# A prefix log-sum-exp on one core: from two consecutive time steps per partition to one, with Exp and Ln issued by pairs of row blocks

## The chip, the core and the metric

The kernel runs on one core of a Trainium2 chip. Its engines work side by side and meet only at semaphores: TensorE (PE, matmul, with its weight loads as PEld), VectorE (DVE), ScalarE (ACT, which evaluates Exp and Ln), GpSimd (POOL) and SyncE (SP); the last two issue the transfers here. The metric is the device time of one execution in microseconds (us). The kernel before takes 1290.47 us, the median of three runs (1289.72 to 1290.6). All durations below come from one profiled execution of it, unless something else is said.

## The reference

The input x has shape 4 x 4096 x 4128 (batch, time, feature), float32. Along time the reference keeps a running log of a sum of exponentials, for each batch and feature by itself:

```python
out[:, 0, :] = x[:, 0, :].copy()
for t in range(1, S):
    mx = np.maximum(out[:, t - 1, :], x[:, t, :])
    out[:, t, :] = mx + np.log(np.exp(out[:, t - 1, :] - mx) + np.exp(x[:, t, :] - mx))
```

So out[t] = log(exp(x[0]) + ... + exp(x[t])). The input is 270.5 MB, the output as much.

## The kernel before

The kernel computes exp(x), then a prefix sum over time, then the logarithm. It works in blocks of 256 time steps by all 4128 features, 64 blocks in all: 16 blocks for each of the 4 batches. A block lies in SBUF as a tile `xt` of 128 partitions x 2 x 4128: partition p holds the time steps 2p and 2p+1, which are neighbours in memory, so a transfer moves one run of 33,024 bytes per partition. SP issues the load (L134).

ACT turns the whole tile into fp16 exponentials `et` with one instruction of 8256 elements (L138). `scan` then handles the *preceding* block. The features are cut into four chunks of 1024 columns and a tail of 32. For each chunk one PSUM tile `pt` (128 x 1024 float32; the pool `pmain` has three) is filled by matmuls of 512 columns, all recorded at L79 since a helper `mm` issues them. The matmul contracts over partitions, so a triangular matrix as weights makes a prefix sum over time. `head(c)` adds `incl` times the even steps, `excl` times the odd steps and, except in the first block of a batch, `last` times `carry[c]`. That is the sum up to each even step. Ln of it goes into `xt` (L97). `second(c)` adds `ident` times the odd steps into the same `pt`, which makes the sum up to each odd step. Ln of that goes into `xt` too (L104), and DVE copies `pt` to fp16 as the new `carry[c]` (L105). `last` picks row 127 of the carry, the sum up to the end of the block. The tail has a PSUM tile `qt` of its own, one Ln for both steps (L123) and one copy (L124). POOL then issues the store of `xt` to the output (L125): the result is written over x in the same tile. `xt` has five buffers, so a load waits for the store that empties its buffer.

The order on each engine is the program's own order (`manual_schedule`). Inside a block it is head(0), head(1), second(0), head(2), second(1), head(3), second(2), tail matmuls, second(3), tail Ln. On ACT one period is therefore: Exp of block k+1, then eight Ln of 1024 columns and the tail Ln of block k. [...] each period has two ACT_TABLE_LOAD.

A copy at L105 waits for the Ln that reads the same `pt`, and the next matmul into that buffer waits for the copy.

Of the kernel before, what the change touches and what calls it, by code (L numbers as in the profile page):

```python
# [1 line left out]

# [4 lines left out]

FP32 = mybir.dt.float32
FP16 = mybir.dt.float16
ACT = mybir.ActivationFunctionType  # L10
P = 128
R = 2
CH = 1024
MM = 512


def _constants(nc, pool):


    def tri(base, name):  # L20
        t = pool.tile([P, P], FP16, name=name)
        nc.gpsimd.memset(t, 1.0)

        nc.gpsimd.affine_select(
            out=t, in_=t, pattern=[[1, P]], compare_op=mybir.AluOpType.is_ge,
            fill=0.0, base=base, channel_multiplier=-1,
        )
        return t

    def ones_where_zero(base, mult, step, name):  # L30
        t = pool.tile([P, P], FP16, name=name)
        nc.gpsimd.memset(t, 0.0)
        nc.gpsimd.affine_select(  # L33
            out=t, in_=t, pattern=[[step, P]], compare_op=mybir.AluOpType.not_equal,
            fill=1.0, base=base, channel_multiplier=mult,
        )
        return t

    return (
        tri(0, "incl"),  # L40
        tri(-1, "excl"),
        ones_where_zero(0, 1, -1, "ident"),
        ones_where_zero(-(P - 1), 1, 0, "last"),
    )


@with_exitstack
def kernel(
    ctx: ExitStack,
    tc: tile.TileContext,  # L50
    x: bass.AP,
    out: bass.AP,
):

    nc = tc.nc
    B, S, D = x.shape
    rows = P * R
    n_t = S // rows  # L60
    assert S % rows == 0
    n_main = D // CH
    tail = D - n_main * CH
    t0 = n_main * CH

    consts = ctx.enter_context(tc.tile_pool(name="consts", bufs=1))
    incl, excl, ident, last = _constants(nc, consts)

    xpool = ctx.enter_context(tc.tile_pool(name="xpool", bufs=5))
    epool = ctx.enter_context(tc.tile_pool(name="epool", bufs=2))  # L70
    cpool = ctx.enter_context(tc.tile_pool(name="cpool", bufs=1))
    pmain = ctx.enter_context(tc.tile_pool(name="pmain", bufs=3, space=bass.MemoryType.PSUM))
    ptail = ctx.enter_context(tc.tile_pool(name="ptail", bufs=2, space=bass.MemoryType.PSUM))

    carry = [cpool.tile([P, CH], FP16, name=f"carry{c}") for c in range(n_main)]
    carry_t = cpool.tile([P, tail], FP16, name="carry_t") if tail else None

    def mm(pt, w, rhs, start, stop):
        nc.tensor.matmul(pt, lhsT=w, rhs=rhs, start=start, stop=stop, skip_group_check=True)  # L79

    def scan(b, k, xt, et):
        first = k == 0

        def head(c):
            pt = pmain.tile([P, CH], FP32, name="pt")
            for s in range(0, CH, MM):
                o = pt[:, s:s + MM]
                seg = slice(c * CH + s, c * CH + s + MM)
                mm(o, incl, et[:, 0, seg], True, False)
            for s in range(0, CH, MM):  # L90
                o = pt[:, s:s + MM]
                seg = slice(c * CH + s, c * CH + s + MM)
                mm(o, excl, et[:, 1, seg], False, first)
            if not first:
                for s in range(0, CH, MM):
                    mm(pt[:, s:s + MM], last, carry[c][:, s:s + MM], False, True)
            nc.scalar.activation(xt[:, 0, c * CH:(c + 1) * CH], pt, ACT.Ln)  # L97
            return pt

        def second(c, pt):  # L100
            for s in range(0, CH, MM):
                seg = slice(c * CH + s, c * CH + s + MM)
                mm(pt[:, s:s + MM], ident, et[:, 1, seg], False, True)
            nc.scalar.activation(xt[:, 1, c * CH:(c + 1) * CH], pt, ACT.Ln)  # L104
            nc.vector.tensor_copy(carry[c], pt)  # L105

        prev = None
        for c in range(n_main):
            pt = head(c)
            if prev is not None:  # L110
                second(c - 1, prev)
            prev = pt
        if tail:
            qt = ptail.tile([P, R, tail], FP32, name="qt")
            seg = slice(t0, D)
            for j in range(R):
                mm(qt[:, j, :], incl, et[:, 0, seg], j == 0, False)
                mm(qt[:, j, :], incl if j else excl, et[:, 1, seg], False, first)
                if not first:
                    mm(qt[:, j, :], last, carry_t, False, True)  # L120
        second(n_main - 1, prev)
        if tail:
            nc.scalar.activation(xt[:, :, t0:D], qt, ACT.Ln)  # L123
            nc.vector.tensor_copy(carry_t, qt[:, 1, :])  # L124
        nc.gpsimd.dma_start(  # L125
            out=out[b, k * rows:(k + 1) * rows, :].rearrange("(p j) d -> p j d", j=R), in_=xt,
        )

    ctx.enter_context(tc.manual_schedule())
    work = [(b, k) for b in range(B) for k in range(n_t)]  # L130
    pending = None
    for b, k in work:
        xt = xpool.tile([P, R, D], FP32, name="xt")
        nc.sync.dma_start(  # L134
            out=xt, in_=x[b, k * rows:(k + 1) * rows, :].rearrange("(p j) d -> p j d", j=R),
        )
        et = epool.tile([P, R, D], FP16, name="et")
        nc.scalar.activation(et, xt, ACT.Exp)  # L138
        if pending is not None:
            scan(*pending)  # L140
        pending = (b, k, xt, et)
    scan(*pending)


# [1 line left out]
_INS = ['x']  # L146
_OUTS = [((4, 4096, 4128), 'float32')]


# [23 lines left out]
```

## Time and profile before

| what | value |
|---|---|
| median of three runs | 1290.47 us |
| the profiled execution: its own time, and its span | 1290.47 us, 1288.7 us |
| ACT busy | 1117.1 us, 87% of the span |
| PE busy | 624.2 us, 48% |
| DVE busy | 313.8 us, 24% |
| moved by DMA | 541.48 MB, mean 420 GB/s |
| first Exp starts, first Ln starts | 13.38 us, 31.54 us |
| third and last Exp start | 41.49 us, 1246.09 us |
| last Ln ends | 1273.10 us |

The span runs from the first to the last instruction, and the execution's own time is 1.8 us longer. "Busy" counts the time in which an engine executes; matmuls are pipelined and their ends are modelled, so a busy PE is not a PE at its peak. The granted clock (PEclk) is the share of its full speed that PE was allowed. A line such as "L105" is a line of the kernel.

### The profile page before, as it was taken

The page shows a single profiled execution, that of the slowest core. Times are in us where ns is not written, and L with a number is a line of the kernel's source. Part 1 is how long each engine was busy: PE and PEld are TensorE (multiplying, and loading weights), DVE is VectorE, ACT ScalarE, POOL GpSimd, SP SyncE. Part 2 cuts the span into 40 slices and gives each one's busy share as a digit, 9 for nine tenths or more (in the row PEclk, how much of TensorE's full clock was granted, in tenths as well). Part 3 has the DMA queues.
Part 4 walks back from the last instruction along what each step waited for, and adds up shares of the span by engine and source line. Part 5 has one row for each costly group of instructions (what it writes and reads, how often), then busy time and mean ns, then how long its engine had stood idle before and what let it go on. Part 6 is the DMA issues. An engine that isn't in the chain of part 4 may idle for free.

```text
span 1288.7 us, 6563 instructions
## 1 busy us (share of the span) xinstructions
PE 624.2 (48%) x2392; PEld 246.8 (19%) x2392; DVE 313.8 (24%) x320; ACT 1117.1 (87%) x766; POOL 36.0 (3%) x76
## 2 busy tenths in 40 slices
PE   1544644545446446455455464464553544644543
PEld 0211211212112112122122121121221211211211
DVE  0322312223223122132232231222222322312223
ACT  5889899898898898998998989989989889889894
POOL 0000000000000000000000000000000000000000
PEclk9877778778677777786777777777867777778777
DMA  9999999999999999999999999999999999999966
GB/s 407 417 415 431 433 419 429 433 422 428 434 432 429 423 426 429 422 434 428 426 426 433 424 431 431 434 432 430 427 432 424 426 435 429 432 421 432 430 299 263
DMA packets 18464, 541.48 MB, mean 420 GB/s; under 512 B 2048, under 2 KB 2048, under 8 KB 2048
## 3 DMA queue, kind: packets, MB, share of 16 engines
q0 software_dynamic: 9216, 270.54, 49.3%
q1 hardware_dynamic: 9216, 270.54, 49.0%
q8 instruction: 18, 0.29, 0.1%
q14 instruction: 14, 0.11, 0.0%
HBM read 270.53 MB, written 270.53 MB: 420 GB/s over the span
## 4 chain that ended last, share of the span: by engine, by line
ACT 60%; PE 35%; issue 2%; DMA 2%; DVE 0%; DVEq 0%; SPq 0%; ACTq 0%
PE pt L79 35%; ACT et L138 34%; ACT xt L97 11%; ACT L97 6%; ACT L138 6%; ACT xt L104 2%; DMA xt<-in_x_dram 2%; ACT xt L123 1%; DVE carry L105 0%; DVEq L168 0%; SPq L134 0%; DVE carry_t L124 0%; ACTq L97 0%; DVEq L124 0%
## 5 line engine op out<-in xcount | busy, mean ns | idle before, releaser
L105 DVE CAST carry<-pt 128x1024 f16<-128x1024 f32 x256 | 307.5, 1222 | 960.8 <-ACT xt L104 960.8
L79 PE MATMUL pt<-et,ident 128*128 128x512 f16 x512 | 202.2, 486 | 606.4 <-ACT xt L97 606.4
L138 ACT ACTIVATE et<-xt 128x8256 f16<-128x8256 f32 x64 | 453.3, 7082 | 14.7 <-DMA xt<-in_x_dram 14.0
L97 ACT ACTIVATE xt<-pt 128x1024 f32<-128x1024 f32 x256 | 255.2, 1022 | 126.6 <-PE pt L79 125.8
L104 ACT ACTIVATE xt<-pt 128x1024 f32<-128x1024 f32 x256 | 254.9, 1026 | 11.7 <-PE pt L79 11.7
L79 PE MATMUL pt<-et,incl 128*128 128x512 f16 x512 | 200.7, 482 | 41.2 <-DVE carry L105 20.7
L79 PE MATMUL pt<-et,excl 128*128 128x512 f16 x512 | 193.7, 468 | 0.0
L79 PEld LDWEIGHTS <-ident 128*128 128x128 f16 x512 | 55.7, 109 | 684.8 <-issue 660.3
L79 PE MATMUL pt<-carry,last 128*128 128x512 f16 x480 | 166.4, 433 | 0.0
L79 PEld LDWEIGHTS <-incl 128*128 128x128 f16 x704 | 75.5, 114 | 155.9 <-issue 121.3
L79 PEld LDWEIGHTS <-excl 128*128 128x128 f16 x576 | 66.8, 116 | 101.2 <-issue 57.4
L138 ACT ACT_TABLE_LOAD x63 | 80.8, 1283 | 1.9 <-PEq L157 0.8
L97 ACT ACT_TABLE_LOAD x63 | 80.8, 1283 | 1.1
L79 PEld LDWEIGHTS <-last 128*128 128x128 f16 x600 | 64.9, 110 | 82.6 <-issue 46.6
L125 POOL DMA_DIRECT2D out_dram<-xt x64 | 34.2, 534 | 1237.3 <-ACT xt L123 1237.3
L79 PE MATMUL qt<-et,incl 128*128 128x32 f16 x192 | 17.9, 178 | 0.0
L123 ACT ACTIVATE xt<-qt 128x64 f32<-128x64 f32 x64 | 16.0, 251 | 0.0
L79 PE MATMUL qt<-carry_t,last 128*128 128x32 f16 x120 | 15.1, 176 | 0.0
L124 DVE CAST carry_t<-qt 128x32 f16<-128x32 f32 x64 | 11.6, 181 | 0.0
L79 PE MATMUL qt<-et,excl 128*128 128x32 f16 x64 | 11.3, 177 | 0.0
L33 POOL TENSOR_SCALAR_AFFINE_SELECT ident<-ident 128x128 f16<-128x128 f16 x1 | 0.3, 288 | 0.0
L33 POOL TENSOR_SCALAR_AFFINE_SELECT last<-last 128x128 f16<-128x128 f16 x1 | 0.3, 288 | 0.0
(10 smaller groups left out, 1.8 us busy)
## 6 DMA issues: line engine op xcount, KB each, us to landing
xt<-in_x_dram SPq DMA_DIRECT2D x64, 4128.0 KB, 24.3
out_dram<-xt POOLq DMA_DIRECT2D x64, 4128.0 KB, 23.6
```

What stands on the lines that cost most here:

```text
L33: nc.gpsimd.affine_select(out=t, in_=t, pattern=[[step, P]], compare_op=mybir.AluOpType.not_equal, fill=1.0, base=base, channel_multiplier ...
L79: nc.tensor.matmul(pt, lhsT=w, rhs=rhs, start=start, stop=stop, skip_group_check=True)
L97: nc.scalar.activation(xt[:, 0, c * CH:(c + 1) * CH], pt, ACT.Ln)
L104: nc.scalar.activation(xt[:, 1, c * CH:(c + 1) * CH], pt, ACT.Ln)
L105: nc.vector.tensor_copy(carry[c], pt)
L123: nc.scalar.activation(xt[:, :, t0:D], qt, ACT.Ln)
L124: nc.vector.tensor_copy(carry_t, qt[:, 1, :])
L125: nc.gpsimd.dma_start(out=out[b, k * rows:(k + 1) * rows, :].rearrange("(p j) d -> p j d", j=R), in_=xt,)
L138: nc.scalar.activation(et, xt, ACT.Exp)
```

## The change

A block is now 128 time steps, one per partition, so a tile is 128 x 4128, a transfer moves one run of 16,512 bytes per partition, and there are 128 blocks (32 for each batch). `excl` and `ident` are gone: `incl` times `et` plus `last` times `carry` is the whole sum. A `pt` is filled once by four matmuls, read by one Ln and by one copy to the carry. To keep the number of table loads, two blocks form a group: ACT does two Exp, then the eight Ln and two tail Ln of the preceding group. `xt` has eight buffers of half the size, `et` five. `pmain` keeps three buffers. Stores are issued after each block of 128.

```diff
-R = 2
+G = 2
...
-    rows = P * R
+    rows = P
...
-    xpool = ctx.enter_context(tc.tile_pool(name="xpool", bufs=5))
-    epool = ctx.enter_context(tc.tile_pool(name="epool", bufs=2))
+    xpool = ctx.enter_context(tc.tile_pool(name="xpool", bufs=8))
+    epool = ctx.enter_context(tc.tile_pool(name="epool", bufs=5))
...
-        def head(c):
+        for c in range(n_main):
             pt = pmain.tile([P, CH], FP32, name="pt")
             for s in range(0, CH, MM):
-                o = pt[:, s:s + MM]
                 seg = slice(c * CH + s, c * CH + s + MM)
-                mm(o, incl, et[:, 0, seg], True, False)
-            for s in range(0, CH, MM):
-                o = pt[:, s:s + MM]
-                seg = slice(c * CH + s, c * CH + s + MM)
-                mm(o, excl, et[:, 1, seg], False, first)
+                mm(pt[:, s:s + MM], incl, et[:, seg], True, first)
             if not first:
                 for s in range(0, CH, MM):
                     mm(pt[:, s:s + MM], last, carry[c][:, s:s + MM], False, True)
-            nc.scalar.activation(xt[:, 0, c * CH:(c + 1) * CH], pt, ACT.Ln)
-            return pt
-
-        def second(c, pt):
-            for s in range(0, CH, MM):
-                seg = slice(c * CH + s, c * CH + s + MM)
-                mm(pt[:, s:s + MM], ident, et[:, 1, seg], False, True)
-            nc.scalar.activation(xt[:, 1, c * CH:(c + 1) * CH], pt, ACT.Ln)
+            nc.scalar.activation(xt[:, c * CH:(c + 1) * CH], pt, ACT.Ln)
             nc.vector.tensor_copy(carry[c], pt)
...
         if tail:
-            qt = ptail.tile([P, R, tail], FP32, name="qt")
...
+            qt = ptail.tile([P, tail], FP32, name="qt")
+            mm(qt, incl, et[:, t0:D], True, first)
+            if not first:
+                mm(qt, last, carry_t, False, True)
+            nc.scalar.activation(xt[:, t0:D], qt, ACT.Ln)
+            nc.vector.tensor_copy(carry_t, qt)
+        nc.gpsimd.dma_start(out=out[b, k * rows:(k + 1) * rows, :], in_=xt)
...
-    pending = None
-    for b, k in work:
-        xt = xpool.tile([P, R, D], FP32, name="xt")
...
+    pending = []
+    for g in range(0, len(work), G):
+        group = []
+        for b, k in work[g:g + G]:
+            xt = xpool.tile([P, D], FP32, name="xt")
+            nc.sync.dma_start(out=xt, in_=x[b, k * rows:(k + 1) * rows, :])
+            et = epool.tile([P, D], FP16, name="et")
+            nc.scalar.activation(et, xt, ACT.Exp)
+            group.append((b, k, xt, et))
+        for p in pending:
+            scan(*p)
+        pending = group
+    for p in pending:
+        scan(*p)
```

More of the change, by code (lines that the diff above doesn't have):

```diff
@@ L40, in _constants @@
         tri(0, "incl"),
-        tri(-1, "excl"),
-        ones_where_zero(0, 1, -1, "ident"),
         ones_where_zero(-(P - 1), 1, 0, "last"),
@@ L66 @@
     consts = ctx.enter_context(tc.tile_pool(name="consts", bufs=1))
-    incl, excl, ident, last = _constants(nc, consts)
-    xpool = ctx.enter_context(tc.tile_pool(name="xpool", bufs=5))
-    epool = ctx.enter_context(tc.tile_pool(name="epool", bufs=2))
+    incl, last = _constants(nc, consts)
+    xpool = ctx.enter_context(tc.tile_pool(name="xpool", bufs=8))
+    epool = ctx.enter_context(tc.tile_pool(name="epool", bufs=5))
     cpool = ctx.enter_context(tc.tile_pool(name="cpool", bufs=1))
@@ L107, in scan @@
[L107 to L112, printed above, removed]
-        if tail:
-            qt = ptail.tile([P, R, tail], FP32, name="qt")
[L115 to L127, printed above, removed]
+            nc.scalar.activation(xt[:, c * CH:(c + 1) * CH], pt, ACT.Ln)
+            nc.vector.tensor_copy(carry[c], pt)
+        if tail:
+            qt = ptail.tile([P, tail], FP32, name="qt")
[4 more added lines that the diff above has]
+            nc.vector.tensor_copy(carry_t, qt)
@@ L129 @@
+        nc.gpsimd.dma_start(out=out[b, k * rows:(k + 1) * rows, :], in_=xt)
     ctx.enter_context(tc.manual_schedule())
     work = [(b, k) for b in range(B) for k in range(n_t)]
-    pending = None
-    for b, k in work:
-        xt = xpool.tile([P, R, D], FP32, name="xt")
[L134 to L141, printed above, removed]
@@ L142 @@
-    scan(*pending)
+    pending = []
[12 more added lines that the diff above has]
+        scan(*p)
```

## The prediction

> **What bounds the kernel now.** I read the page first. ACT is busy for 87% of the span and the DMA engines for over 90% in nearly every slice, so either could be the bound.
>
> ```profile
> DMA  9999999999999999999999999999999999999966
> ACT 60%; PE 35%; issue 2%; DMA 2%; DVE 0%; DVEq 0%; SPq 0%; ACTq 0%
> L105 DVE CAST carry<-pt 128x1024 f16<-128x1024 f32 x256 | 307.5, 1222 | 960.8 <-ACT xt L104 960.8
> L138 ACT ACTIVATE et<-xt 128x8256 f16<-128x8256 f32 x64 | 453.3, 7082 | 14.7 <-DMA xt<-in_x_dram 14.0
> L97 ACT ACTIVATE xt<-pt 128x1024 f32<-128x1024 f32 x256 | 255.2, 1022 | 126.6 <-PE pt L79 125.8
> ```
>
> The chain that ended last is ACT and PE; DMA has 2% of it. A group line gives busy us, mean ns of one instruction, then the idle time before it and its releaser. Next, the waits (total us, times, longest):
>
> ```profile
> ACT xt L97 <- PE pt L79: 125.8, 113, 1.5
> ACT et L138 <- DMA xt<-in_x_dram: 14.0, 2, 11.3
> ```
>
> An Exp waits for a load only twice, both at the start. So loads come in time, and a period is set by ACT and its waits for PE. One period in order of time (start, duration; idle before in brackets):
>
> ```profile
> 594.50 7.08 ACT L138 ACTIVATE et<-xt 128x8256 f16<-128x8256 f32 x1
> ...
> 602.90 1.94 ACT L97 ACTIVATE xt<-pt 128x1024 f32<-128x1024 f32 x2
> 603.97 1.01 PE L79 MATMUL pt<-et,ident 128*128 128x512 f16 x2 [9.05 <-ACT xt L97]
> ...
> 607.58 1.02 ACT L97 ACTIVATE xt<-pt 128x1024 f32<-128x1024 f32 x1 [1.54 <-PE pt L79]
> ...
> 610.46 1.02 ACT L97 ACTIVATE xt<-pt 128x1024 f32<-128x1024 f32 x1 [0.94 <-PE pt L79]
> ...
> 612.43 2.36 DVE L105 CAST carry<-pt 128x1024 f16<-128x1024 f32 x2 [1.66 <-ACT xt L104]
> ```
>
> Three `pt` are filled during Exp, so the Ln phase starts at once, then ACT waits for refills. Two Ln in a row take 1.94, so the second adds 0.92; two copies take 2.36, so the second adds 1.14. Early in the burst two matmuls of 512 take 1.06 (0.43 apart), later 0.59 (0.215 apart): PE is cold after the 9 us of Exp. Whole periods (length, PE busy, granted clock, DMA share, GB/s) show what that costs:
>
> ```profile
> 614.74:635.10 20.36, 10.49 (x39) 0.75 1.01 430
> 635.10:653.94 18.84, 8.42 (x36) 0.82 1.01 421
> 653.94:673.48 19.54, 8.76 (x32) 0.74 1.00 426
> ```
>
> ACT issues the same work in each, yet the length moves with the granted clock. The Exp starts give the repeating sequence 18.84, 19.54, 20.00, 20.24, 20.36. In the clock's own record it changes only at multiples of 3.413 us: cold 0.5, warm 1.0. It turns warm at the end of a window in which PE had work for over about 0.765 (0.76 didn't, 0.77 did) and cold after an idle one.
>
> **What the Trainium skill says.** "TensorE: Matmul & The Clock Gate", Part 1 (What's actually happening), has a free-running window of 3413 ns after which a busy PE goes from half to full clock; this trace agrees. "PSUM — Partial Sum Buffer", PSUM bank collisions raise a hardware error, says that two engines, two readers included, must not touch one bank at once. That is why a copy follows its Ln; the copies here start 0.04 us after it. "DMA: Bandwidth & Descriptors", Why small descriptors are slow, names about 3 cycles per packet, so halving 33 KB rows should cost little. Here a row of 33,024 bytes holds an engine 1.222 us, and the trace's few 8,192-byte packets mostly 0.309 us: about 0.007 us each beyond the bytes.
>
> **The change, part by part (per 256 steps; before against after).**
>
> *ACT.* Exp: a 1024 Ln takes 1.022 and the 8256 Exp 7.082, about 0.838 ns an element, so an Exp of 4128 takes about 3.64; two, overlapping by 0.10, take 7.18, or +0.10. Ln: still eight. Tail: one of 64 (0.245) becomes two of 32 at about 0.215, +0.09 with overlap. Table loads: still two. Bare ACT period: about +0.2 us.
>
> *PE.* 32 matmuls of 512 before (8 each of `incl`, `excl`, `last`, `ident`), 32 after (16 `incl`, 16 `last`); tails 6 to 4. No saving.
>
> *DVE.* Eight copies of 1.222 where there were four, +4.9 us: 9.3 us back to back with both tail copies. Before, a buffer served two Ln for one copy. Now each Ln has a copy behind it that holds the buffer: the Ln phase becomes paced by refill, Ln, copy round three buffers.
>
> *The Ln phase, step by step.* Let 0 be the start of the first Exp. Exp end at 7.18, table load 7.19 to 8.47, three prefilled Ln start at 8.49, 9.41 and 10.33. Copies end at 10.77, 11.91 and 13.05. PE starts chunk 4 at 10.83, when the first buffer is free. Cold, four matmuls issue in 1.71, and the last lands 0.16 later.
> - chunk 4 lands 12.70, Ln 12.73 (could start 11.25: waits 1.48); the tail Ln follows at 13.65.
> - chunk 5 starts on PE at 12.59, lands 14.46, Ln 14.49 (waits 0.72).
> - chunk 6 starts 14.30, lands 16.17, Ln 16.20 (waits 0.79).
> - If PE is warm from about 16.1, chunk 7 starts 16.01 and lands 17.07, Ln 17.12; chunk 8 waits for chunk 5's copy (15.55 to 16.77), lands 17.93, Ln 18.04; no further wait.
> - Tail Ln ends 19.18, table load ends 20.47. Period: 20.48, with 2.99 us of waits where the sampled period before has about 2.7.
>
> PE turns warm 2.61 us (0.765 of a window) to 6.02 us after its burst starts at 10.83, as the burst falls on the windows. Earliest, chunk 5 lands 14.04, and chunks 7 and 8 wait for copies: period about 19.9. Latest, chunk 7 lands 17.45 and chunk 8 18.32: 20.85. Before, the same swing is 18.84 to 20.36.
>
> *Where it settles.* Six windows are 20.48 us. A shorter period starts the next burst earlier against the windows, so warmth comes later in it and the period grows; a longer one does the reverse. Before, even the longest (20.36) is under 20.48, so the phase never rests and the sequence climbs and falls back: mean 19.75 ((1246.09 - 41.49) / 61). After, 20.48 lies between 19.9 and 20.85, where the drift stops, with warmth 5.2 us after the burst starts. The period should lock there. The first blocks of a batch, without carry matmuls, disturb it for a few periods, with no net sum.
>
> *DMA.* Sixteen rows of 1.222 per engine become 32 of about 0.615: 19.55 to about 19.7 us bare; measured with its stalls the mix ran at 421 to 430 GB/s, so 8.454 MB take 19.7 to 20.1 and about 0.1 more after. It hides under 20.48. The buffers hold four groups, not five, but stores leave in halves and the load behind each starts sooner. POOL and SP issue 128 transfers instead of 64; an issue takes 0.53 and 0.33, and neither queue holds compute.
>
> *Ends.* First Exp: half of the load's 9.78 us, 13.38 - 4.89 = 8.5. Four Exps paced by loads of 4.9: the fourth runs 23.2 to 26.8, first Ln at 28.1 (before 31.54); an Ln phase and table load of about 11.6 bring the third group's Exp to 39.7. Plus 61 x 20.48 = 1249.3: last group's Exp at 1289.0. Its predecessor's Ln phase ends 19.2 later, and the last eight chunks follow, paced by copies, in about 10.9: 1319.1. The last store is half as long: 15.6 (1288.7 - 1273.1) less 4.9 is 10.7. Span 1329.8; with 1.8 around it, as in the profiled execution, whose time is the median: 1331.6. I say **1331**.
>
> **Rivals.** *No lock:* the phase keeps drifting between 19.9 and 20.85, mean about 20.3: 61 x 0.18 = 11 less, 1320. For it: before drifts so. Against: 20.48 is well inside my range; my terms would have to be 0.4 too long.
>
> *Slower still:* eight copies beside Ln and matmuls lengthen one another in PSUM, or a 16.5 KB packet costs over 0.64 us, so that DMA is the bound. At 20.8 a period it gives 1331 + 61 x 0.32 = 1350. Against: copies keep 1.22 beside Ln today, and 8 KB packets show little overhead.
>
> *Not slower:* PE stays warm through Exp, because prefills wait for the last copies and shorten its idle stretch. Then chunk 4 lands at 11.8, the copy chain alone sets about 19.0, and DMA at 19.7 becomes the bound: 1331 - 61 x 0.78 = 1283. The last prefill starts after the last copy, at about 0.3 us of the next period, and lasts 1.1 at most; the next burst is at 10.83, so over 9 us of idleness remain, over two windows. It decides from a period of 19.9 downward, where the 8 us saved at the ends are spent; I don't expect it.
>
> *The change doesn't do what it says:* ACT, PE and DVE orders are fixed by hand, so no.
>
> **How the numbers follow.** Lock 0.73 (own range 1325 to 1338), no lock 0.13, slower still 0.09, not slower 0.05. Leaving out the fast rival and part of the slow one, the range is 1309 to 1347. About 0.2% (2.6 us) is what the measurement tells from no change. Faster 0.04, same 0.02, slower 0.94: only the third rival ends at or below 1293.
>
> **What would show it.** Right: Exp starts 20.48 apart for long stretches; ACT waiting for PE near 3 us a group (1.5, then twice 0.7 to 0.8); DVE near 650 us; the mean clock near 0.75; no Exp waiting for a load after the start. Wrong: periods near 19.7 with Exp waiting for loads; a clock at 1.0 during Exp; copies well over 1.22; Ln waits spread over all five refilled chunks.

## The result, and the profile after

The kernel after takes 1327.99 us (median of four runs, 1326.83 to 1329.16) against 1290.24 us, now the median of four runs of the kernel before: a ratio of 1.0293, 95% interval 1.0275 to 1.0311, so 38 us slower. The prediction was 1331, with 1309 to 1347 as its range.

The page of the kernel after, the lines that answer to those shown of before:

```profile
DMA  9999999999999999999999999999999999999986
ACT 56%; PE 26%; DVE 12%; issue 3%; DMA 2%; DVEq 0%; SPq 0%; ACTq 0%
L89 DVE CAST carry<-pt 128x1024 f16<-128x1024 f32 x512 | 601.7, 1219 | 703.1 <-ACT xt L88 702.8
L88 ACT ACTIVATE xt<-pt 128x1024 f32<-128x1024 f32 x512 | 499.9, 1023 | 169.4 <-PE qt L76 88.5
L108 ACT ACTIVATE et<-xt 128x4128 f16<-128x4128 f32 x128 | 459.5, 3635 | 11.0 <-DMA xt<-in_x_dram 10.3
```

Each copy costs what it cost before (1219 ns, 1222 before), and there are twice as many. DVE, which had 0% of the chain that ended last, now has 12% of it. The total wait of the Ln instructions rose from 138.3 us (126.6 at L97 and 11.7 at L104) to 169.4 us. Exp still waits for loads only at the start.

The waits of the kernel after (total us, times, longest) show the new link of the chain:

```profile
PE pt L76 <- DVE carry L89: 647.6, 138, 15.6
ACT xt L88 <- PE qt L76: 88.5, 78, 1.4
ACT xt L88 <- ACT xt L95: 44.2, 60, 1.0
ACT xt L88 <- PE pt L76: 34.8, 59, 1.4
ACT et L108 <- DMA xt<-in_x_dram: 10.3, 4, 6.5
```

Before, PE waited for Ln (606.4 us) and for copies only 20.7 us. Now it waits for copies. The second and third lines are waits for PE as well: the releaser named is the last event seen, a tail matmul or a tail Ln that came just before, while the instruction that waits is a 1024 Ln whose chunk was being filled. One Ln phase in order of time (kernel after):

```profile
640.17 2.85 ACT L88 ACTIVATE xt<-pt 128x1024 f32<-128x1024 f32 x3
641.22 3.48 DVE L89 CAST carry<-pt 128x1024 f16<-128x1024 f32 x3 [9.16 <-ACT xt L88]
642.50 1.01 PE L76 MATMUL pt<-et,incl 128*128 128x512 f16 x2 [9.46 <-DVE carry L89]
...
644.40 1.02 ACT L88 ACTIVATE xt<-pt 128x1024 f32<-128x1024 f32 x1 [1.38 <-PE qt L76]
...
646.21 1.02 ACT L88 ACTIVATE xt<-pt 128x1024 f32<-128x1024 f32 x1 [0.70 <-ACT xt L95]
...
647.87 2.85 ACT L88 ACTIVATE xt<-pt 128x1024 f32<-128x1024 f32 x3 [0.63 <-PE pt L76]
```

Three prefilled Ln, then waits of 1.38, 0.70 and 0.63 us, then three Ln in a row once PE is warm. PE's burst starts only when the first copy has ended, 2.33 us after the first Ln; before, it started 1.07 us after it. Two whole periods (length, PE busy, granted clock, DMA share, GB/s):

```profile
631.68:652.13 20.45, 10.22 (x38) 0.75 1.01 416
652.13:672.59 20.46, 9.60 (x34) 0.75 1.01 412
```

The 38 us can be followed in the two profiled executions, whose spans are 1288.7 and 1325.0, so 36.3 apart (the profiled execution of the kernel after is the fastest of its four). From the third group's Exp to the last group's there are 61 periods: 1246.09 - 41.49 = 1204.60 before, 1287.03 - 40.36 = 1246.67 after, which is 42.1 more, or 0.69 a period (19.75 to 20.44). The start is 1.1 shorter, and the stretch from the last Exp's start to the end is 38.0 instead of 42.6. 42.1 - 1.1 - 4.6 = 36.4, the difference of the spans but for rounding.

### The profile page after: what moved, and what is told of

Its sections match the earlier page's. It is cut to its first block, busy times and chain, and to the rows that moved or that the text cites. A ratio compares the mean times of both kernels' runs of the same rounds, so it can differ in the third digit from the quotient of the medians.

```text
span 1325.0 us, 7395 instructions
## 1 busy us (share of the span) xinstructions
PE 640.3 (48%) x2268; PEld 243.2 (18%) x2268; DVE 614.0 (46%) x640; ACT 1132.5 (85%) x894; POOL 69.3 (5%) x136
## 4 chain that ended last, share of the span: by engine, by line
ACT 56%; PE 26%; DVE 12%; issue 3%; DMA 2%; DVEq 0%; SPq 0%; ACTq 0%
ACT et L108 34%; PE pt L76 26%; DVE carry L89 12%; ACT xt L88 10%; ACT L88 6%; ACT L108 6%; DMA xt<-in_x_dram 2%; ACT xt L95 0%; PE qt L76 0%; SPq L106 0%; DVEq L140 0%; DVEq L89 0%; ACTq L88 0%
## 5 line engine op out<-in xcount | busy, mean ns | idle before, releaser
L89 DVE CAST carry<-pt 128x1024 f16<-128x1024 f32 x512 | 601.7, 1219 | 703.1 <-ACT xt L88 702.8
L76 PE MATMUL pt<-et,incl 128*128 128x512 f16 x1024 | 390.2, 471 | 674.4 <-DVE carry L89 647.6
L88 ACT ACTIVATE xt<-pt 128x1024 f32<-128x1024 f32 x512 | 499.9, 1023 | 169.4 <-PE qt L76 88.5
L108 ACT ACTIVATE et<-xt 128x4128 f16<-128x4128 f32 x128 | 459.5, 3635 | 11.0 <-DMA xt<-in_x_dram 10.3
L76 PE MATMUL pt<-carry,last 128*128 128x512 f16 x992 | 373.8, 466 | 0.0
L76 PEld LDWEIGHTS <-incl 128*128 128x128 f16 x1152 | 123.0, 111 | 868.8 <-issue 819.5
L76 PEld LDWEIGHTS <-last 128*128 128x128 f16 x1116 | 129.2, 116 | 202.6 <-issue 124.4
L97 POOL DMA_DIRECT2D out_dram<-xt x128 | 68.2, 533 | 1246.8 <-ACT xt L95 1239.4
L95 ACT ACTIVATE xt<-qt 128x32 f32<-128x32 f32 x128 | 25.3, 198 | 0.0
L96 DVE CAST carry_t<-qt 128x32 f16<-128x32 f32 x128 | 23.1, 181 | 0.0
```

Source lines behind the costliest of these rows:

```text
L88: nc.scalar.activation(xt[:, c * CH:(c + 1) * CH], pt, ACT.Ln)
L95: nc.scalar.activation(xt[:, t0:D], qt, ACT.Ln)
L96: nc.vector.tensor_copy(carry_t, qt)
L97: nc.gpsimd.dma_start(out=out[b, k * rows:(k + 1) * rows, :], in_=xt)
```

## Experiments

The theory: an Ln phase is paced by three PSUM buffers going round through cold refill, Ln and copy, and PE's clock windows then hold the period at six windows, 20.48 us. Its rivals: work that simply adds up; the number of DVE copies as such; the shorter runs and doubled number of transfers. Labels beginning with b_ start from the kernel before, those with a_ from the kernel after.

### Is the period held by the clock windows?

One short Ln was added to each of the two kernels, nothing else.

```diff
# b_ln1
-            nc.scalar.activation(xt[:, :, t0:D], qt, ACT.Ln)
+            for _ in range(2):
+                nc.scalar.activation(xt[:, :, t0:D], qt, ACT.Ln)
# a_ln1
-            nc.scalar.activation(xt[:, t0:D], qt, ACT.Ln)
+            for _ in range(2):
+                nc.scalar.activation(xt[:, t0:D], qt, ACT.Ln)
```

> The kernel before with its tail Ln done twice (the second writes the same values), 0.245 us less 0.10 of overlap: about 0.145 us more ACT work in each of 64 periods. If a period simply adds up, the time rises by 64 x 0.145 = 9 us, to about 1299. If the period is held by the clock windows, the longest period, 20.36, now reaches 20.48 and rests there for long stretches: mean period about 20.3, and 1318 to 1330, three to four times the work added.

> The kernel after with each tail Ln done twice, about 0.10 us more per block after overlap, 0.2 us per group of two. If a period simply adds up: 64 x 0.2 = 13 us more, 1341. If the period is locked to six clock windows: still 20.48, 1327 to 1331.

Measured: 1325.21 us for b_ln1, ratio to the kernel before 1.0272 (1.0257 to 1.0287), and 1330.31 us for a_ln1, 1.0312 (1.0297 to 1.0328). Three whole periods of b_ln1 (same columns as above):

```profile
548.99:569.46 20.47, 10.34 (x39) 0.75 1.01 412
569.46:589.94 20.48, 10.35 (x39) 0.75 1.00 413
589.94:610.42 20.48, 10.35 (x39) 0.75 1.01 416
```

The page of b_ln1 shows 30.0 us of tail Ln where before had 16.0. So at most 14 us of work cost 36 us, and the same kind of work cost the kernel after 2 us. Work that adds up can't do both. The periods of b_ln1 climb from 19.3 (18.6 in the first batch) through 19.9, 20.2 and 20.3 to 20.48 and stay there; their mean is 20.29. The kernel before was 0.12 us short of this rest point, and nearly all of the change's loss can be had from it with one Ln a block.

The granted clock shows the hold itself. Take a burst, the run of matmuls after PE's long idle stretch. The time from its first matmul to the moment at which the clock rises from 0.50 to 1.00 is called the delay here. Three such cold stretches, the first with the warm stretch behind it (length, PE busy, granted clock, DMA share, GB/s):

```profile
642.50:647.80 5.30, 5.30 (x15) 0.50 1.00 427
647.80:658.04 10.24, 4.92 (x23) 1.00 1.00 385
624.36:627.76 3.40, 3.40 (x10) 0.50 1.00 413
643.53:649.55 6.02, 5.10 (x14) 0.50 1.00 406
```

The first two are of the kernel after, the third of a_ln1, the last of a_4buf below. Where the periods rest at 20.48, the delay is the same from group to group: 5.38 us in the kernel after, 5.74 in b_ln1, 3.39 in a_ln1. In a_ln1 most groups of a batch pass, at 20.53, before this point is reached. The added work thus brought the warm clock earlier in the burst, and the rest point stayed at 20.48. In the kernel before no delay gives 20.48: 2.72, 4.36, 5.30, 5.78 and 6.02 us go with periods of 18.84, 19.54, 20.01, 20.24 and 20.36, over and over.

### What sets the length of the period?

PE was kept at work through the Exp, in both kernels:

```diff
# a_warm; b_warm has the same after head(1)
-    ptail = ctx.enter_context(tc.tile_pool(name="ptail", bufs=2, space=bass.MemoryType.PSUM))
+    ptail = ctx.enter_context(tc.tile_pool(name="ptail", bufs=1, space=bass.MemoryType.PSUM))
+    pwarm = ctx.enter_context(tc.tile_pool(name="pwarm", bufs=1, space=bass.MemoryType.PSUM))
+    wt = pwarm.tile([P, MM], FP32, name="wt")
...
+            if lead and c == 2:
+                for _ in range(40):
+                    mm(wt, incl, et[:, 0:MM], True, True)
```

> The kernel after with 40 idle matmuls of 512 columns (into a spare PSUM bank, nobody reads them) after the three prefills of each group, so that PE has work all through the Exp; the tail keeps one PSUM buffer instead of two. If the cold clock sets the 20.48, the period falls until the transfers bind, 19.7 to 20.0: 1282 to 1302, PE's clock 1.0, and Exp begins to wait for loads. If doubled copies on DVE or the shorter runs cost the time, whatever the clock: 1320 or more.

> The kernel before with 40 idle matmuls per block after the prefills, and one PSUM buffer for the tail instead of two. If the transfers stand right behind ACT and PE, at about 19.7 a block: 1283 to 1290, with Exp now waiting for loads. If the cold clock is the only bound before, the period falls to 18.4 and the time to about 1210.

Measured: a_warm 1286.36 us, ratio 0.9971 (0.9959 to 0.9982); b_warm 1283.59 us, 0.9948 (0.9936 to 0.9961). The kernel after gains 42 us from matmuls that nobody reads, and ends 0.3% ahead of the kernel before. Both then meet the transfers. ACT in a stretch before this and in one after, in b_warm (length, ACT busy, granted clock, DMA share, GB/s):

```profile
41.37:59.71 18.34, 17.41 (x13) 1.00 1.03 422
600.00:700.00 100.00, 88.51 (x61) 0.98 1.00 432
```

The early periods of b_warm are 18.34 us, until the prefetched blocks are used up; from then on they are about 19.75, and Exp waits for loads 53 times, 84.3 us in all, 14 of them at the start. In a_warm it waits 39 times, 35.8 us. The mean period of the kernel before was 19.75 too, so the early periods are nearly all that b_warm could gain.

To see the chain without this, a quarter of the output was stored, with and without the idle matmuls:

```diff
-        nc.gpsimd.dma_start(out=out[b, k * rows:(k + 1) * rows, :], in_=xt)
+        nc.gpsimd.dma_start(out=out[b, k * rows:(k + 1) * rows, 0:CH], in_=xt[:, 0:CH])
```

> The kernel after storing only columns 0 to 1023 of each block, so a quarter of the output; all compute as after. If transfers had a share in the 20.48, or a store frees its buffer late: clearly under 1320. If ACT and PE hold the period: 20.4 to 20.5 still, and only the last store shorter, by about 4 us: 1321 to 1328.

> The kernel with 40 idle matmuls per group, storing only columns 0 to 1023 of each block (a quarter of the output). With PE warm and transfers out of the way the chain of refill, Ln and copy alone should show: period 18.93, the value that its undisturbed groups had with full stores, and 61 x 0.74 = 45 us less than with them: 1235 to 1245. If something else than transfers held the mean of 19.67 there: 1275 or more.

Measured: a_quarter 1321.42 us, 1.0242 (1.0228 to 1.0256); a_warm_quarter 1236.56 us, 0.9584 (0.957 to 0.9599). In a_quarter the DMA row of the page falls from 9 tenths and more to about 7, and the time stays, apart from the shorter last store:

```profile
DMA  9967767777777777777777667777777776776721
```

Its periods average 20.49. In a_warm_quarter nearly all are 18.93, with one of 19.16 in every eight or so. So with PE warm a period takes 18.93 (predicted for the copy chain alone: about 19.0), and cold PE adds 1.5 to that.

### Is it the ring of buffers with the copy in it?

First, a fourth buffer, with the tail taking turns in the same four:

```diff
# a_4buf
-    pmain = ctx.enter_context(tc.tile_pool(name="pmain", bufs=3, space=bass.MemoryType.PSUM))
-    ptail = ctx.enter_context(tc.tile_pool(name="ptail", bufs=2, space=bass.MemoryType.PSUM))
+    pmain = ctx.enter_context(tc.tile_pool(name="pmain", bufs=4, space=bass.MemoryType.PSUM))
...
-            qt = ptail.tile([P, tail], FP32, name="qt")
+            qt = pmain.tile([P, CH], FP32, name="pt")[:, 0:tail]
```

> The kernel after with four buffers of 128x1024 in PSUM instead of three; the tail takes its turn in the same four instead of having two of its own. If the Ln phase is paced by refill, Ln and copy going round three buffers, the waits for PE fall from 2.7 to about 1.5 us a group, the longest period falls under 20.48, the lock is lost and the transfers bind at 19.7 to 20.0: 1282 to 1302. If the number of copies, or the shorter runs, set the time: 1320 or more.

Measured: 1328.15 us, 1.0295 (1.028 to 1.031), a clear miss. Its own order of time gives one reason:

```profile
643.53 0.18 PE L75 MATMUL pt<-et,incl 128*128 128x32 f16 x1 [8.81 <-DVE carry L88]
643.55 0.19 PE L75 MATMUL pt<-carry_t,last 128*128 128x32 f16 x1
644.66 1.01 PE L75 MATMUL pt<-et,incl 128*128 128x512 f16 x2 [0.92 <-DVE carry L88]
...
646.61 1.02 ACT L87 ACTIVATE xt<-pt 128x1024 f32<-128x1024 f32 x1 [1.55 <-issue]
```

The tail's two small matmuls take the first buffer that comes free, the next chunk waits for another copy, and Ln waits 1.55 us again. The other reason is the lock. The fourth buffer did shorten the period at a given delay of the warm clock: with 5.22 us it was 20.09, where the kernel after has 20.45 with 5.23. But from there the periods climbed to 20.48 all the same and rested where the delay is 6.02 us, the latest that the prediction's sum allows. So the time alone would have said that the buffer does nothing. The pair was then run without the tail:

```diff
# a_3notail: the tail's block under "if tail:", its pool and carry_t are gone
# a_4notail: the same, and
-    pmain = ctx.enter_context(tc.tile_pool(name="pmain", bufs=3, space=bass.MemoryType.PSUM))
+    pmain = ctx.enter_context(tc.tile_pool(name="pmain", bufs=4, space=bass.MemoryType.PSUM))
```

> The kernel after without the 32 tail columns: their matmuls, Ln and carry copies are left out, so those columns of the output hold x. It is the base for the four-buffer kernel beside it. About 0.2 us less ACT work a group. Locked, the period stays 20.4 to 20.5: 1323 to 1329. If periods simply add up, 64 x 0.2 = 13 us less: 1315.

> The same without tail columns and with four PSUM buffers of 128x1024 instead of three, so that no tail takes a turn among them. If the ring of three buffers with a copy at its end makes the waits, four chunks are now prefilled and the period falls below 20.48 at every phase, 18.1 to 19.7, until transfers bind at about 19.7: 1280 to 1300, no lock. If only the cold clock matters, or the number of copies: near the kernel with three buffers.

Measured: a_3notail 1328.36 us, 1.0299 (1.0285 to 1.0313); a_4notail 1271.76 us, 0.986 (0.9847 to 0.9874). Dropping the tail alone changed nothing that shows in the time: two Ln a group less, and the period still 20.48, now with a delay of 5.62 us at rest instead of 5.38. The fourth buffer took 57 us off. The waits in a_4notail:

```profile
PE pt L74 <- DVE carry L87: 647.0, 71, 14.7
ACT xt L86 <- PE pt L74: 59.0, 109, 0.7
ACT et L99 <- DMA xt<-in_x_dram: 41.0, 42, 6.5
ACT xt L86 <- ACT xt L86: 30.3, 59, 0.5
```

Ln waits 89.3 us instead of 172.9 in a_3notail, and the transfers have become the bound (42 waits of Exp, periods of 19.76 on average from the twentieth on), though PE is still cold after every Exp (mean clock 0.725). The first line is as long as ever, most of it idle time during Exp, which costs nothing. A complete kernel with four such buffers and one of its own for the tail was not tried.

Then the copy itself was halved, with three buffers:

```diff
# a_halfcopy; the carries are set to zero once at the start
-            nc.vector.tensor_copy(carry[c], pt)
+            nc.vector.tensor_copy(carry[c][:, 0:MM], pt[:, 0:MM])
```

> The kernel after copying only the first 512 of each chunk's 1024 columns to the carry (the other half of the carry stays zero, so half of the columns lose the sum of earlier blocks): a copy takes about 0.69 us instead of 1.22. If the copy's length is part of the ring, periods fall to 18.9 to 20.2, below six windows, the lock is lost and the transfers bind at times: 1275 to 1300. If PE's clock alone makes the waits: still 20.48 and 1323 or more.

Measured: 1273.43 us, 0.9877 (0.9862 to 0.9892), slightly better than expected; no Exp waited for a load after the start. A copy took 0.69 us. Four periods in a row:

```profile
509.28:528.20 18.92, 8.87 (x37) 0.73 1.01 430
528.20:547.67 19.47, 9.51 (x37) 0.74 1.00 422
547.67:567.59 19.92, 10.02 (x37) 0.74 1.01 427
567.59:587.79 20.20, 10.25 (x37) 0.66 1.01 429
```

These climb like those of the kernel before, and fall back: their sum, 78.51 us, is 23 clock windows of 3.413. The number of copies is the same 512 as after, so the number is not the cause. Together with a_4notail, where the copies are whole, this shows that the time for which each holds its buffer is.

### Are the shorter runs to blame?

```diff
# b_16k; the stores likewise
-        nc.sync.dma_start(
-            out=xt, in_=x[b, k * rows:(k + 1) * rows, :].rearrange("(p j) d -> p j d", j=R),
-        )
+        xv = x[b, k * rows:(k + 1) * rows, :].rearrange("(p j) d -> p j d", j=R)
+        for j in range(R):
+            nc.sync.dma_start(out=xt[:, j, :], in_=xv[:, j, :])
```

> The kernel before with each load and each store cut in two, one for the even and one for the odd steps: runs of 16,512 bytes and 128 transfers each way, as after, but all compute as before. If the shorter runs and more transfers cost the 38 us: near 1328. If they are hidden, as the prediction has it: 1288 to 1296, at most about 0.1 us a block more.

> The kernel before with 40 idle matmuls per block and one PSUM buffer for the tail, and with each load and store cut in two for the even and odd steps. Transfers bind as in the kernel with idle matmuls alone (1283.6); the halves bring the last store's end about 2 us earlier, as they did without idle matmuls: 1279 to 1284.

Measured: b_16k 1288.13 us, 0.9986 (0.998 to 0.9993): runs of 16,512 bytes and 128 transfers each way cost the kernel before nothing, and end 2 us sooner. With the idle matmuls as well, b_warm_16k takes 1287.91 us, 0.9986 (0.9979 to 0.9992), a miss: 4 us more than b_warm, where a gain of about 2 was expected. Its third Exp starts 1.1 us later, and where transfers bind its periods are about 19.82 instead of 19.75. So the shorter runs cost a little only where transfers are the bound. Whether it is the extra packets or the strided halves was not tried.

## Why the prediction was right

- *What bounds the kernel.* Right: ACT with its waits for PE. a_quarter shows the same for the kernel after.
- *ACT.* About +0.2 us a period was forecast. ACT's busy total rose by 15.4 us (1117.1 to 1132.5), 0.24 a period; its busy time counts overlaps once. One sum was off: the prediction's own rate gives 3.62 us for the Exp of 4128 (7.082 - 4128 x 0.838 ns), not 3.64. The trace has 3.635, and 7.18 for two, so the written value was the better one by luck.
- *PE and DVE.* No saving on PE; DVE rose to 614.0 us busy. The 650 named as a sign was the plain product without overlap.
- *The Ln phase.* Of the kernel before, the prediction says that three `pt` are filled during Exp. Its trace shows two, filled mostly before it: in the period that starts at 635.10, the last of them is full at 635.52. In the kernel after there are three, as the steps have it. The waits were forecast as 1.48, 0.72 and 0.79 and measured as 1.38, 0.70 and 0.63, on the three chunks named. The starts were hit more closely: 12.72, 14.53 and 16.19 us into the period, against 12.73, 14.49 and 16.20. The waits differ because the forecast counts from the moment at which the next Ln could have started (0.92 after the last one's start), the profile from the last one's end (1.02). a_4notail and a_halfcopy show that buffers and copies make this ring.
- *Where it settles.* Right for three of the four batches: mostly 20.45 to 20.48, with a delay of 5.2 to 5.4 us, where 5.2 was forecast. Not foreseen was a flat stretch: in the first batch ten periods stood at 20.35 while the delay crept from 3.54 to 4.57 us, so there the delay made no difference and nothing held the period. This batch holds practically all of the 2.6 us by which the 61 periods fall short of 61 x 20.48; the mean is 20.44. One group in eight took about 20.63. The lock does not explain the loss by itself: at like delays the period after is longer than before by 1.1 us (2.7), 0.8 (4.4) and 0.45 (5.3), which is the ring's cost. The reading that the length moves with the granted clock was loose: of the three periods shown there, 20.36 has 0.75 and 19.54 has 0.74. It moves with the delay.
- *DMA.* Hidden, as said. The bound was put at 19.7 to 20.1 us a period, and 0.1 more after. Where transfers bind, the periods are about 19.75 in b_warm, 19.82 in b_warm_16k and 19.87 on average from the twentieth on in a_warm, so the forecast was right and the margin under 20.48 was 0.6 to 0.7. A row of 16,512 bytes took 0.615 us (median), as worked out; the part beyond the bytes comes to 0.008 us by the prediction's own two figures, not 0.007.
- *Ends.* The third Exp came at 40.36 (39.7 forecast), the last group's remainder took 28.8 (30.1), and from the last Ln to the end 9.1 us passed (10.7). With the 2.6 above: +0.7 - 1.3 - 1.6 - 2.6 = -4.8, which is 1325.0 measured less the 1329.8 forecast for the span. These are the mis-sized terms.
- *Rivals.* "Not slower" named a warm PE with the transfers as the bound, at 1283. That is what a_warm made on purpose: 1286. It didn't come by itself, since PE stayed idle over 9 us in each Exp.

## What to carry to other kernels

If an engine's clock is granted by windows of fixed length, a loop of nearly a whole number of windows can be pulled to it: look at the list of single periods, not at their mean, and count how far the longest is from the next whole number. In a loop that is held so, neither a small saving nor a small addition shows in the time (a_4buf, a_3notail, a_ln1); a saving that takes it out of the hold shows at once (a_4notail, a_halfcopy). Count for how long each buffer of a ring is held, with every reader behind one another: here a copy behind every Ln came with a loss of 38 us, and a fourth buffer took 57 off in the kernel without tail. And an engine's idle stretch can be worth filling with useless work, as long as the next bound behind it isn't met at once; here it was worth 0.5% to the kernel before.

## What the runs showed that was not expected

- The DMA share was 1.00 or 1.01 in whole periods of the kernel after at 412 to 418 GB/s, and the same share in a_4notail at 431. A full DMA row was thus no sign that the transfers were the bound; the rate and the waits of Exp told them apart.
- In b_ln1 one Ln of 0.23 us a block cost 0.55 us a period, more than twice its own length.
- Every eighth group took about 0.2 us longer in the kernel after and in a_warm_quarter, but not in a_3notail. In these groups of the kernel after, the fifth of the eight long Ln starts 14.81 to 14.83 us into the period, elsewhere at 14.54 or sooner, and the last one follows. A packet of queue q14, which the page calls "instruction", starts within 6 us of that Ln in all eight of them (within 1 us in a_warm_quarter). Whether this is the reason was not tried, so the cause stays open.
